# One written order from the query products to the second group of the attention's output projection, and other task rates

## The chip, the cores and the metric

The kernel runs on one core of one Trainium2 chip. The metric is the device time of one execution in microseconds (us). The kernel before takes 2666.85 us, the median of three runs (2665.67 to 2668.78). The execution that was profiled took 2665.4 us; its trace spans 2663.6 us from the first to the last instruction. All times inside the trace are counted from the start of that span.

## The reference, cut to what matters

One step of a one-layer decoder on 512 prompt tokens and 8 sample (decode) tokens, all in fp32:

```
x += W_out [ norm(RG-LRU group) ; headnorm(mLSTM group) * o ]
x += CrossAttn(RMSNorm(x), memK, memV)      4 heads of 512 over 256 memory tokens
x += W_down relu(RMSNorm(x) W_up)^2
y  = RMSNorm(x)
```

For the prompt tokens the memory's keys and values are products of `mem_prompt` with `w_mk` and `w_mv`. Each of the 8 decode tokens has keys and values of its own, which come ready from the caches `cache_mem_k` and `cache_mem_v`. Both kinds of tokens go together through the weights `w_cq` (queries) and `w_co` (output projection).

## The kernel before, in words

**Tiles.** The 520 tokens are the columns, 128 features the rows of a tile. An fp32 product is made of three matmuls on rounded parts: a weight is cast to a high part `whi` on ScalarE (L129 or L138), and VectorE subtracts to get the low part `wlo` (L130 or L146); activations are split likewise. High and low parts of weights have three buffers each, so the cast for a job waits until TensorE is done with the job three before it.

**Jobs.** A job is one weight block of 128 x 1024 and its matmuls. The list `jobs` holds them in the order in which TensorE makes them. The part that matters here is:

- 32 jobs of the query products (`w_cq`), 4 heads of 4 column blocks of 2 jobs; 48 matmuls each
- 64 jobs of the memory's keys and values: keys and values of head 0, of head 1, keys of heads 2 and 3, values of heads 2 and 3; eight jobs each. The matmuls of one such job take about half the time of a query job. Their cost is given as `MCOST`
- the output projection `w_co`: 4 plain jobs (`plain_pair`, 48 matmuls each), then seven groups of seven products of 24 matmuls (`quad_jobs`, a Strassen-like scheme over 2 x 2 blocks, in the order P1 P2 P6 P5 P7 P3 P4). `n_early` is the number of the first plain job; the first group is `n_early + 4` to `n_early + 10`, the second `n_early + 11` to `n_early + 17`

In a group P1, P6, P7 and P4 add into one PSUM accumulator, P5 and P3 into another. After each product the result so far is added to `x` (L1452), and the next product into the same accumulator waits for that addition. Four weight sums are formed on VectorE in a group (L1310). When a pair of rows of `x` is complete, a task `fact_pair` forms four sums of it for the MLP (L1271, L1272, L1253), and `sums_out` splits and stores them (L1282, L1284). The first `fact_pair` waits seven steps.

**Tasks.** Work beside the jobs is written as generators. `step_tasks` is called once in each job and advances every task:

```
t[2] += 1.0 if t[1] is None else t[1] * cost
while t[2] > 0.999:
    t[2] -= 1.0
    next(t[0])
```

The decode tokens' attention is one such task, `attn_decode_all`, with rate `DRATE`. It walks through 64 items: for each head eight items of keys (L1018) and eight of values (L1025), one per decode token; the order is K0 K1 V0 K2 V1 K3 V2 V3. An item's 512 KB are loaded by GpSimd's queue (L986, L993) four items ahead, and VectorE reduces them: for an item of values, four instructions at L1025. When the last value item of a head is done, the prompt's task of that head (`attn_prompt`) may make its second product, probabilities times values (TensorE, L224), copy the four results out of PSUM (L1217, with the decode columns from `od` at L1218), and split them into `fo` (L799, L800), which the output projection reads. For each pair of them a task `o_sums` forms four differences (L889), splits them (L899, L900) and stores them by GpSimd's queue into `odram` (L902, L903); `block_out` starts it, for the first four pairs with a rate of its own. `o_loads` brings the stored differences back as `to` for the groups of the output projection (L915, SyncE's queue) and makes those of the last two pairs itself (L889, L799, L800). GpSimd's queue also stores the finished memory keys and values; all that it issues goes out in the order in which it is written.

**What sets the order.** In a block `tc.manual_schedule()` each engine issues the block's instructions in the order in which the program writes them. Outside such a block, and between the instructions of two blocks, a planner decides by priorities. In a manual block `run_jobs(..., fixed=True)` writes for job i: the loads, the cast of job i+2, one step of the tasks, the low part of job i+2, the matmuls of job i, the result's evacuation. With `low_first` the low part comes ahead of the tasks' step. In the kernel before there are three such blocks near the change: from the first query job to the second plain job (with the loop that empties the task list), the third and fourth plain job, and the first group. Between the first and the second stand, to the planner, the release of the early SBUF pools, the opening of the late one, four weight loads held back for it, and the start of `o_loads`. From the second group on the planner orders everything but the very last two products.

Of the kernel before, what the change touches and what calls it, by code (L numbers as in the profile page):

```python
# [14 lines left out]
PSUM = bass.MemoryType.PSUM  # L15
# [22 lines left out]
EVAC = 100  # L38
EARLY = 10
PRE = 1  # L40
DRATE = 1.45
MCOST = 0.35


@with_exitstack
def tile_trunk(ctx: ExitStack, tc: tile.TileContext, a, o):
# [9 lines left out]
    early_sb, early_ps = (ctx.enter_context(ExitStack()) for _ in range(2))  # L56
# [3 lines left out]
    late = {}  # L60
# [26 lines left out]
    def halves(t):  # L87
        return t.rearrange("p (h c) -> p h c", h=2)
# [14 lines left out]
    jobs = []  # L103
# [7 lines left out]
    def w_load(i):  # L111
        if "fetch" in jobs[i] or "raw" in jobs[i] or "w" in jobs[i]:
            return
        jobs[i]["raw"] = w_raw(jobs[i]["src"])

    def w_fetch(i):
        if i < len(jobs) and "fetch" in jobs[i]:
            jobs[i]["fetch"]()
# [22 lines left out]
    def w_low(i):  # L141
        if "w" in jobs[i]:
            return
        raw, hi = jobs[i].pop("cast")
        lo = wpool.tile([P, 8, P], F32R, tag="wlo", name=nm("wlo"))
        V.tensor_tensor(out=lo, in0=raw, in1=hi.bitcast(F32), op=ALU.subtract)  # L146
        jobs[i]["w"] = hi, lo

    def start(gen, rate=None):

        tasks.append([gen, rate, 0.0])

    def step_tasks(cost=1.0):
        for t in list(tasks):
# [3 lines that stand above are left out]
                try:  # L158
                    next(t[0])
                except StopIteration:  # L160
                    tasks.remove(t)
                    break

    def run_jobs(first, last, fixed=False, low_first=False):


        n = len(jobs)
        for i in range(first, last):
            with tc.high_priority(offset=AHEAD):
                for k in (i + 3, i + 4)[1 if i else 0:]:  # L170
                    if k < n:
                        w_load(k)
                w_fetch(i + FETCH)
                if i + 2 < n:
                    (w_cast if fixed else w_split)(i + 2)
            j = jobs[i]
            if "pre" in j:
                j["pre"]()
            if low_first:
                w_low(i + 2)  # L180
            step_tasks(j.get("cost", 1.0))
            if fixed and i + 2 < n:
                w_low(i + 2)
            j["mm"](*j.pop("w"))
            if "post" in j:
                with tc.high_priority(offset=EVAC):
                    j["post"]()
        while last == n and tasks:
            step_tasks()
# [602 lines left out]
    def pair_slot(name):  # L792
        return slot(name, (P, 2, HT), F32R)

    def split_to(out, src, g=None):

        hi, lo = out[:, 0], out[:, 1]
        if g is None:
            S.copy(hi, src)  # L799
            V.tensor_tensor(out=lo, in0=src, in1=hi.bitcast(F32), op=ALU.subtract)  # L800
        else:
            S.activation(hi, src, AF.Copy, scale=g)
            V.scalar_tensor_tensor(out=lo, in0=src, scalar=g, in1=hi.bitcast(F32),
                                   op0=ALU.mult, op1=ALU.subtract)
# [66 lines left out]
    o_even, o_last = {}, []  # L871

    def block_out(t, n):
        fo[n] = [pair_slot("fo") for _ in range(2)]
        for hf in range(2):
            split_to(fo[n][hf], t[:, HALF[hf]])
        i = n // 2
        if n % 2 == 0:
            o_even[i] = t
        elif i < 6:  # L880
            start(o_sums(i, o_even.pop(i), t, i < 4), 2.2 if i < 4 else None)
        else:
            o_last.append((i, o_even.pop(i), t))

    def diffs(t0, t1):

        b11, b12, b21, b22 = t0[:, HALF[0]], t0[:, HALF[1]], t1[:, HALF[0]], t1[:, HALF[1]]
        for j, out, p, q in ((4, b11, b12, b11), (5, b12, b22, b12), (6, b22, b22, b11), (7, b21, b21, b22)):
            V.tensor_tensor(out=out, in0=p, in1=q, op=ALU.subtract)  # L889
            yield j, out  # L890

    def o_sums(i, t0, t1, slowly):

        for n, _ in enumerate(diffs(t0, t1)):
            if n == 3 or slowly and n == 1:
                yield
        for t, js in ((t1, (7, 6)), (t0, (4, 5))):
            hi = pair_slot("oh")
            S.copy(hi, halves(t))  # L899
            V.tensor_tensor(out=halves(t.bitcast(F32R)), in0=halves(t), in1=hi.bitcast(F32), op=ALU.subtract)  # L900
            for k, j in enumerate(js):
                stream_load(odram[i][j - 4, :, 0], hi[:, k].bitcast(F32))  # L902
                stream_load(odram[i][j - 4, :, 1], t[:, HALF[k]])  # L903
            if slowly:
                yield

    def o_loads():

        for i in range(KB // 2):
            to[i][1], to[i][2], to[i][3] = fo[2 * i][0], fo[2 * i + 1][0], fo[2 * i + 1][1]  # L910

        def fetch(j):
            for i in range(len(odram)):
                to[i][j] = pair_slot("to")
                load(to[i][j].bitcast(F32), odram[i][j - 4])  # L915

        def make(j, of):
            for i, d, got in of:
                while j not in got:
                    k, x = next(d)  # L920
                    got[k] = x
                to[i][j] = pair_slot("to")
                split_to(to[i][j], got[j])

        last = [(i, diffs(t0, t1), {}) for i, t0, t1 in o_last]
        o_last.clear()
        fetch(6)
        make(6, last[0:1])
        yield
        make(6, last[1:2])  # L930
        fetch(4)
        yield
        make(4, last)
        fetch(5)
        yield
        make(5, last)
        yield
        fetch(7)
        make(7, last)
# [6 lines left out]
    def ev_q(h, j):  # L946
        def ev(ps):
# [5 lines left out]
            if h == 0 and j == 3:  # L953
                start(attn_decode_all(), DRATE)
            if h == 0 and j == 0:
# [132 lines left out]
    def split_later(parts):  # L1088

        for t, hi, lo in parts:  # L1090
            yield
            S.copy(hi, t)
            V.tensor_tensor(out=lo, in0=t, in1=hi.bitcast(F32), op=ALU.subtract)

    def mk_jobs(h, j):
# [3 lines left out]
        def mm(g, wh, wl):  # L1099
            if g == 0:  # L1100
                box["ps"] = mm_tile()[:, 0, 0:NMEM]
            for i in range(8):
                k = g * 8 + i
                xh, xl = mact[k]
                for wi, (w, x) in enumerate(((wh, xh), (wh, xl), (wl, xh))):
                    PE.matmul(box["ps"], w[:, i, :], x, start=(k == 0 and wi == 0),  # L1106
                              stop=(k == KB - 1 and wi == 2))

        def post():
# [7 lines left out]
            if j == 3:  # L1117
                start(attn_prompt(h))
        js = [dict(src=a["w_mk"][n, g], cost=MCOST, mm=lambda wh, wl, g=g: mm(g, wh, wl)) for g in range(2)]
        js[-1]["post"] = post  # L1120
        return js

    def mv_jobs(h):
# [16 lines left out]
        def post():  # L1140
# [5 lines left out]
            start(split_later(mvx[h]))  # L1146
        js = [dict(src=a["w_mv"][h, g], cost=MCOST, mm=lambda wh, wl, g=g: mm(g, wh, wl)) for g in range(8)]
        js[-1]["post"] = post
# [490 lines left out]
    n_early = len(jobs)  # L1639
    jobs += projection("w_co", dx[0], dx[1], "ssf", fo, to, x2_done, fact_split, False)  # L1640

    held = [jobs[n_early + 4 + i].pop("fetch") for i in range(2)]
# [18 lines left out]
    with tc.manual_schedule():  # L1661
        run_jobs(n_cq, n_early + 2, True)
        while tasks:
            step_tasks()
    early_sb.close()
    late["sb"] = ctx.enter_context(tc.tile_pool(name="late", bufs=2, reuse_waits="tile"))
    for fetch in held:
        fetch()
    start(o_loads())
    with tc.manual_schedule():  # L1670
        run_jobs(n_early + 2, n_early + 4, True, True)
    early_ps.close()
    late["mm"] = ctx.enter_context(tc.tile_pool(name="lmm", bufs=3, space=PSUM, reuse_waits="tile"))
    late["aux"] = ctx.enter_context(tc.tile_pool(name="laux", bufs=2, space=PSUM, reuse_waits="tile"))
    with tc.manual_schedule():
        run_jobs(n_early + 4, n_early + 11, True, True)
    run_jobs(n_early + 11, len(jobs) - 2)
    assert not tasks
    with tc.manual_schedule():
        finish(*jobs[-2:])  # L1680
# [103 lines left out]
```

## Time and profile before

| what | value |
|---|---|
| median of three runs | 2666.85 us (2665.67 to 2668.78) |
| profiled execution | 2665.4 us, span 2663.6 us |
| TensorE busy (matmul) | 2627.0 us, 99% |
| VectorE busy | 2219.9 us, 83% |
| ScalarE busy | 1296.9 us, 49% |
| query products | 749 to 936 us |
| memory keys and values | 936 to 1168 us |
| plain jobs of the output projection, rest of the attention | 1168 to 1204 us |
| its first group | 1204 to about 1234 us |

TensorE is busy nearly everywhere, so what a change in this part of the kernel is worth is read from the few places where TensorE waits, or where its granted clock is below full speed. In the rows a matmul's own time is about 0.28 us, but they overlap: their starts stand 0.12 us apart for 260 columns and 0.23 us for 512. The same holds, less strongly, for VectorE and ScalarE, so the distance of two starts is what an instruction costs its engine.

### The profile page before, as it was taken

How to read it: one execution, taken by the hardware profiler on the slowest of the kernel's cores; microseconds unless marked ns; L12 is line 12 of the kernel's file. 1: busy time of each engine (PE TensorE's matmuls, PEld its weight loads, DVE VectorE, ACT ScalarE, POOL GpSimd, SP SyncE). 2: the span in 40 equal slices, each digit the busy share in tenths (PEclk: the TensorE clock that was granted, in tenths of full speed). 3: DMA queues.
4: the chain of work that ended last, by engine and by line, in shares of the span. 5: the costliest groups of instructions: out<-in, count | busy, mean ns of one | idle time of the engine just before them, and what ended most of it. 6: DMA issues, size and time to landing. Idle time of an engine off the chain costs nothing.

```text
span 2663.6 us, 52729 instructions
## 1 busy us (share of the span) xinstructions
PE 2627.0 (99%) x21250; PEld 2589.5 (97%) x21250; DVE 2219.9 (83%) x3729; ACT 1296.9 (49%) x1779; POOL 134.1 (5%) x232
## 2 busy tenths in 40 slices
PE   9999999999999999998999999999999999999997
PEld 9999999999999998988999999999999999999997
DVE  6787685887864568878999999999999988998898
ACT  5646455553453245544575555555553333333344
POOL 0010000000001213320000000000000000000001
PEclk9999999999999999999999999999999999999999
DMA  5354353576456778877687565565579666555642
GB/s 205 106 187 152 112 169 103 175 240 223 141 182 202 275 266 302 293 254 269 224 273 243 199 213 185 199 212 188 196 244 330 216 223 216 183 169 191 211 132 89
DMA packets 243847, 545.43 MB, mean 205 GB/s; under 512 B 26015, under 2 KB 98367, under 8 KB 243603
## 3 DMA queue, kind: packets, MB, share of 16 engines
q1 hardware_dynamic: 222354, 468.55, 51.8%
q0 software_dynamic: 21248, 73.51, 8.0%
q8 instruction: 167, 2.74, 0.4%
q14 instruction: 78, 0.63, 0.1%
HBM read 436.39 MB, written 105.72 MB: 204 GB/s over the span
## 4 chain that ended last, share of the span: by engine, by line
PE 87%; issue 4%; DVE 4%; DMA 2%; ACT 1%; POOL 0%; SPq 0%; POOLq 0%; DVEq 0%; ACTq 0%
PE mm L1340 51%; PE mm L205 22%; PE mm L1137 3%; PE aux L1340 2%; PE aux L224 2%; PE mm L1106 2%; PE mm L1383 2%; DVE wlo L146 1%; PE aux L730 0%; DMA wraw<-in_w_mk 0%; PE aux L663 0%; PE aux L659 0%; DMA wraw<-in_w_in 0%; DMA hc<-r 0%; DMA A<-in_w_co 0%
## 5 line engine op out<-in xcount | busy, mean ns | idle before, releaser
L129 ACT CAST whi<-wraw 128x1024 fp32r<-128x1024 f32 x392 | 411.9, 1051 | 633.1 <-PE mm L1340 414.4
L1340 PE MATMUL mm<-ha,whi 128*128 128x260 f32 x3584 | 644.1, 283 | 2.1 <-DVE X L1521 1.1
L130 DVE TENSOR_TENSOR wlo<-wraw,whi 128x1024 fp32r<-128x1024 f32 x392 | 478.3, 1220 | 120.1 <-ACT whi L129 118.4
L1340 PEld LDWEIGHTS mm<-ha,whi 128*128 128x128 f32 x3584 | 551.0, 188 | 3.0 <-DVE X L1521 1.5
L1340 PE MATMUL mm<-ha,wlo 128*128 128x260 f32 x1792 | 505.1, 282 | 0.6 <-DVE wlo L130 0.6
L1340 PE MATMUL mm<-ta,whi 128*128 128x260 f32 x2320 | 418.6, 282 | 0.0
L1340 PEld LDWEIGHTS mm<-ta,whi 128*128 128x128 f32 x2320 | 355.9, 188 | 0.0
L1340 PEld LDWEIGHTS mm<-ha,wlo 128*128 128x128 f32 x1792 | 337.1, 188 | 1.0 <-DVE wlo L130 1.0
L1340 PE MATMUL mm<-ta,wlo 128*128 128x260 f32 x1160 | 326.4, 281 | 0.0
L1340 PE MATMUL mm<-fa,whi 128*128 128x260 f32 x1488 | 268.6, 282 | 0.0
L205 PE MATMUL mm<-xh,whi 128*128 128x260 f32 x1280 | 265.0, 287 | 0.0
L205 PE MATMUL mm<-xl,whi 128*128 128x260 f32 x1280 | 259.1, 283 | 0.0
L205 PE MATMUL mm<-xh,wlo 128*128 128x260 f32 x1280 | 258.1, 282 | 0.0
L129 ACT CAST whi<-A 128x1024 fp32r<-128x1024 f32 x138 | 144.9, 1050 | 193.2 <-PE mm L1340 143.0
L1340 PEld LDWEIGHTS mm<-fa,whi 128*128 128x128 f32 x1488 | 228.5, 188 | 0.0
L138 ACT CAST whi<-wraw 128x1024 fp32r<-128x1024 f32 x104 | 109.0, 1050 | 238.4 <-PE mm L205 76.9
L1340 PEld LDWEIGHTS mm<-ta,wlo 128*128 128x128 f32 x1160 | 218.4, 188 | 0.0
L1340 PE MATMUL mm<-fa,wlo 128*128 128x260 f32 x744 | 209.4, 281 | 0.0
L1521 DVE TENSOR_TENSOR X<-mm,X 128x260 f32<-128x260 f32 x448 | 170.8, 421 | 42.0 <-PE mm L1340 40.5
L205 PEld LDWEIGHTS mm<-xh,whi 128*128 128x128 f32 x1280 | 198.5, 188 | 1.4
L205 PEld LDWEIGHTS mm<-xh,wlo 128*128 128x128 f32 x1280 | 198.2, 189 | 0.2
L205 PEld LDWEIGHTS mm<-xl,whi 128*128 128x128 f32 x1280 | 197.8, 189 | 0.3
(439 smaller groups left out, 5236.1 us busy)
## 6 DMA issues: line engine op xcount, KB each, us to landing
ha<-hc SPq DMA_DIRECT2D x224, 260.0 KB
wraw<-in_w_in SPq DMA_DIRECT2D x80, 512.0 KB
wraw<-in_w_up SPq DMA_DIRECT2D x66, 512.0 KB
wraw<-in_w_down SPq DMA_DIRECT2D x64, 512.0 KB
A<-in_w_down SPq DMA_DIRECT2D x64, 512.0 KB
A<-in_w_up SPq DMA_DIRECT2D x62, 512.0 KB
hc<-hhi SPq DMA_DIRECT2D x32, 910.0 KB
hc<-r SPq DMA_DIRECT2D x32, 910.0 KB
```

Source lines behind the costliest of these rows:

```text
L129: S.copy(hi, raw)
L130: V.tensor_tensor(out=lo, in0=raw, in1=hi.bitcast(F32), op=ALU.subtract)
L138: S.copy(hi, raw)
L146: V.tensor_tensor(out=lo, in0=raw, in1=hi.bitcast(F32), op=ALU.subtract)
L205: PE.matmul(ps[:, hf, 0:HT], w[:, j, :], x[:, HALF[hf]], start=(k == 0 and wi == 0), stop=(k == n - 1 and wi == 2))
L224: PE.matmul(out, u, v, start=first and i == 0, stop=last and i == 2)
L1106: PE.matmul(box["ps"], w[:, i, :], x, start=(k == 0 and wi == 0), stop=(k == KB - 1 and wi == 2))
L1137: PE.matmul(box["ps"][:, i], x[:, ms], w[:, j], start=(k == 0 and wi == 0), stop=(k == KB - 1 and wi == 2))
L1340: PE.matmul(out, w[:, j, :], x[:, b], start=(new and k == 0 and wi == 0), stop=(p == LAST[acc] and k == per - 1 and wi == 2), skip_group_c ...
L1383: PE.matmul(ps[mp][:, hf, 0:HT], w[:, j, :], x[hf][:, b], start=(kp == 0 and j == 0 and wi == 0), stop=(kp == 1 and j == 7 and wi == 2))
L1521: V.tensor_tensor(out=x, in0=c, in1=x, op=ALU.add)
```

## The change

`DRATE` goes from 1.45 to 1.6 and `MCOST` from 0.35 to 0.32, the rate of the first four `o_sums` tasks from 2.2 to 2.5. The steps of the decode task in a query job (cost 1) go from 1.45 to 1.6; in a job of the memory's keys or values from 0.5075 to 0.512; those of the `o_sums` tasks there from 0.77 to 0.80. The three manual blocks become one, which takes in what stood between them and goes on through the second group (to `n_early + 17`).

```
-DRATE = 1.45
-MCOST = 0.35
+DRATE = 1.6
+MCOST = 0.32
...
-            start(o_sums(i, o_even.pop(i), t, i < 4), 2.2 if i < 4 else None)
+            start(o_sums(i, o_even.pop(i), t, i < 4), 2.5 if i < 4 else None)
...
         run_jobs(n_cq, n_early + 2, True)
         while tasks:
             step_tasks()
-    early_sb.close()
-    late["sb"] = ctx.enter_context(tc.tile_pool(name="late", bufs=2, reuse_waits="tile"))
-    for fetch in held:
-        fetch()
-    start(o_loads())
-    with tc.manual_schedule():
+        early_sb.close()
+        late["sb"] = ctx.enter_context(tc.tile_pool(name="late", bufs=2, reuse_waits="tile"))
+        for fetch in held:
+            fetch()
+        start(o_loads())
         run_jobs(n_early + 2, n_early + 4, True, True)
-    early_ps.close()
-    late["mm"] = ctx.enter_context(tc.tile_pool(name="lmm", bufs=3, space=PSUM, reuse_waits="tile"))
-    late["aux"] = ctx.enter_context(tc.tile_pool(name="laux", bufs=2, space=PSUM, reuse_waits="tile"))
-    with tc.manual_schedule():
-        run_jobs(n_early + 4, n_early + 11, True, True)
-    run_jobs(n_early + 11, len(jobs) - 2)
+        early_ps.close()
+        late["mm"] = ctx.enter_context(tc.tile_pool(name="lmm", bufs=3, space=PSUM, reuse_waits="tile"))
+        late["aux"] = ctx.enter_context(tc.tile_pool(name="laux", bufs=2, space=PSUM, reuse_waits="tile"))
+        run_jobs(n_early + 4, n_early + 18, True, True)
+    run_jobs(n_early + 18, len(jobs) - 2)
```

## The prediction

> **What bounds the kernel now.** I read the page's first lines, then the busy times of the stages from the query products to the end of the output projection, then who TensorE (PE) waited for there.
>
> ```profile
> span 2663.6 us, 52729 instructions
> PE 2627.0 (99%) x21250; PEld 2589.5 (97%) x21250; DVE 2219.9 (83%) x3729; ACT 1296.9 (49%) x1779; POOL 134.1 (5%) x232
> ```
> ```profile
> core 0: us, PE busy (x) PEld busy (x) DVE busy (x) ACT busy (x) POOL busy (x), PEclk, DMA share, GB/s
> 749.00:936.00 187.00, 187.00 (x1560) 186.44 (x1559) 102.58 (x236) 61.19 (x89) 25.77 (x39) 1.00 0.63 216
> 936.00:1168.00 232.00, 226.83 (x1461) 203.05 (x1460) 180.62 (x431) 115.84 (x205) 59.82 (x99) 1.00 0.82 282
> 1168.00:1204.00 36.00, 32.50 (x221) 30.63 (x220) 30.12 (x89) 15.90 (x42) 12.12 (x22) 0.91 0.69 236
> 1204.00:1237.00 33.00, 25.88 (x194) 25.50 (x193) 24.75 (x38) 16.29 (x25) 0.00 (x0) 0.84 0.98 344
> 1237.00:1254.00 17.00, 16.75 (x140) 16.75 (x141) 16.97 (x24) 9.27 (x11) 0.00 (x0) 1.00 0.69 223
> 1254.00:1355.00 101.00, 101.00 (x847) 101.00 (x846) 97.40 (x139) 63.68 (x88) 0.00 (x0) 1.00 0.68 226
> ```
> ```profile
> 1168.33 0.64 PE L1383 MATMUL mm<-fo,whi 128*128 128x260 f32 x4
> 1192.15 1.76 PE L1383 MATMUL mm<-fo,whi 128*128 128x260 f32 x4 [3.47 <-ACT fo L799]
> 1203.82 0.43 PE L1340 MATMUL mm<-fo,whi 128*128 128x260 f32 x2
> 1216.55 0.77 PE L1340 MATMUL mm<-to,whi 128*128 128x260 f32 x2 [6.81 <-ACT to L799]
> ```
> ```profile
> 1191.00:1198.00 7.00, 5.85 (x24) 5.54 (x25) 5.97 (x16) 5.11 (x17) 3.98 (x8) 0.52 0.97 331
> 1211.00:1222.00 11.00, 5.45 (x25) 5.48 (x26) 8.57 (x17) 6.37 (x12) 0.00 (x0) 0.53 0.98 345
> ```
> ```profile
> 1165.70 2.79 PE aux L224 x12
> 1237.25 117.67 PE mm L1340 x982
> ```
>
> PE has nothing to give beside the queries (187 of 187 us). Where the change acts, it waits 3.47 us for the last `fo` and 6.81 us ahead of the first group's P6, and after either wait its clock is granted at half (0.52 and 0.53).
>
> I count from T0 = 1168.33, the first plain product. A matmul of 260 columns costs 117.67/982 = 0.12 us, so a plain job (48) 5.75, a product of a group (24) 2.88, and head 3's probabilities times values (24 of L224) 2 x 2.79 = 5.6. From T0 to P1 (1203.82) 35.5 us pass for 4 x 5.75 + 5.6 = 28.6 of work: 6.9 lost, 3.47 in the wait, most of the rest by the half clock behind it. Group 2 ends at 1237.25 + (982 - 5 x 168) x 0.12 = 1254.3. From P1 on that is 50.4 us for 14 x 2.88 = 40.3: 10.1 lost, 6.81 waiting, some 2.5 by the clock. **17.0 us** is all that can be won here.
>
> **What holds PE.** VectorE's queue.
>
> ```profile
> 1189.91 0.42 DVE L1025 CUSTOM_DVE_ANT_0 kv<-kv,kv 128x256 f32<-128x256 f32 x1
> ...
> 1191.29 1.30 DVE L900 TENSOR_TENSOR o<-o,oh 128x520 fp32r<-128x520 f32 x2
> ...
> 1199.14 1.22 DVE L1310 TENSOR_TENSOR A<-A,A 128x1024 f32<-128x1024 f32 x1
> ...
> 1209.87 0.69 DVE L1444 TENSOR_TENSOR xr<-mm,xr 128x520 f32<-128x520 f32 x1
> 1211.35 1.11 DVE L1253 TENSOR_TENSOR r<-r 128x260 f32<-128x260 f32 x3 [0.80 <-ACT r L1272]
> 1213.58 1.24 DVE L1284 TENSOR_TENSOR r<-r,hhi 128x1040 fp32r<-128x1040 f32 x1 [1.12 <-ACT hhi L1282]
> 1214.74 0.69 DVE L268 TENSOR_TENSOR ssf<-ssf,sq 128x520 f32<-128x520 f32 x1
> 1215.35 0.76 DVE L800 TENSOR_TENSOR to<-o,to 128x260 fp32r<-128x260 f32 x2
> 1216.03 0.42 DVE L1452 TENSOR_TENSOR x<-mm,x 128x260 f32<-128x260 f32 x1
> 1216.37 1.21 DVE L146 TENSOR_TENSOR wlo<-A,whi 128x1024 fp32r<-128x1024 f32 x1
> 1217.50 0.76 DVE L800 TENSOR_TENSOR to<-o,to 128x260 fp32r<-128x260 f32 x2
> ```
>
> The last decode item ends at 1191.3 = T0+23.0, and `fo` of head 3 stands behind it. P6 starts at 1216.55, just behind the end of P1's addition (L1452, 1216.45), not behind L799, which the row names: P6 adds to the same accumulator. Ahead of that addition stand L1253 and L1284, the first `fact_pair`, which the planner drew forward from the second group; they wait on ScalarE by turns (0.80, 1.12). Starts in these rows price VectorE's work: 260 columns 0.34, 520 columns 0.61, 1024 (a weight's low part or a weight sum) 1.13, L1284 1.16, an item of values 1.38.
>
> **Part 1, the rates.** By the rule of `step_tasks`, each query job after the decode task's start makes 1.6 steps in place of 1.45; 24 such jobs make 3.6 steps more, of which the wait for each head's query rows swallows some: 26 items are done at the end of the queries, in place of 24. They cost 2 x 1.38 = 2.8 us beside a VectorE that is busy 102.58 of 187 us; without that cover they would cost PE those 2.8. Beside keys and values the rate stays (0.5075 to 0.512), so the lead of two items persists. Its main effect is that head 2's last item falls in the second of the last eight value jobs, not in the sixth: its product, four copies, eight splits into `fo`, and the differences of pairs 4 and 5 move from the first plain jobs and the loop behind them into those value jobs. Head 3's last item moves only one step, from the third to the second of the emptying loop.
>
> I wrote down VectorE's queue for that order. In the last five value jobs it can't begin head 2's `fo` before TensorE's product: half of that (2.8) and four jobs of 12 matmuls (2.8 each, as L224) lie behind the job that frees ScalarE, 13.9 us ahead of T0; a cast, a copy and a split there make it 11.5. Then come items 57 and 58 (2.8), eight splits (2.7), eight differences (2.7), two L900 (1.2), four low parts (4.5), and some 2.7 waiting for ScalarE's copies: 16.6, so it is 5.1 us late at T0. Items 59 to 63 (6.9), two L900, two halves of head 3's values (1.2), two low parts (2.3) follow: item 63 ends at T0+16.7, where before it was T0+23.0. Two prices:
> - TensorE is ready for head 3's product at T0+11.5, but the halves of its values come at T0+12.2 and, behind item 62, T0+15.3: it waits 3.3 us.
> - The `fo` wait of 3.47 and its half clock go: the plain job that needs `fo` then starts at T0+20.4 and comes to it at T0+23.3; it is there from T0+17.9.
>
> P1 starts at 28.6 + 3.3 = T0+31.9. This part loses 3.3 in place of 6.9.
>
> **Part 2, one order.** `fact_pair` 0 goes back to its own place, steps 8 to 11, in group 2. The path to P6 is now: the last plain job ends at T0+31.9; sum into `xr` 0.65, ScalarE's square and L268 1.3, then the two weight sums of P6 (L1310, 1.13 each and a wait between), which the planner had put ahead at 1199 and which now stand where they are written; the cast, the low part, two splits, P1's addition.
>
> ```profile
> L138 ACT CAST whi<-wraw 128x1024 fp32r<-128x1024 f32 x9 | 9.3, 1049 | 10.0 <-PE mm L1383 4.9 <-DVE wraw L1310 2.0 <-PE mm L1340 1.6
> ...
> L1282 ACT CAST hhi<-r 128x1040 fp32r<-128x1040 f32 x6 | 6.3, 1058 | 2.3 <-DVE r L1253 2.3
> ```
>
> That is 0.7 + 1.3 + 2.5 + 1.05 + 1.15 + 0.7 + 0.4 = 7.8 and some 0.3 of handing over: T0+40.0, where P6 is due at T0+37.6. P6 loses 2.4, P7 and P3 of the group 1.4 in the same way (a weight sum, a cast, a low part, an addition). Group 1: 3.9.
>
> Group 2 now holds `fact_pair` 0 and 1. VectorE's sum there: seven low parts and four weight sums 12.4, seven additions 2.4, two L268 1.2, twice four sums and an L1284 5.0: 21.0 us beside 20.1 of TensorE, and in written order it must also wait for ScalarE's casts about 1 us each time. By the queue: P6 2.4, P7 0.7, P3 2.1, in all 5.3; before, the planner lost 0.25 there (16.75 of 17). At its end VectorE is 4 us late.
>
> **Sum.** 3.3 + 3.9 + 5.3 = 12.5 in place of 17.0.
>
> **What the trace doesn't show, from both sides.** Items 62 and 63 are loaded from GpSimd's queue, in the new order behind the stores of pairs 4 and 5; 63 is issued at about T0+11.8 (pair 5's first L900 ends at T0+7.2, then eight stores of 0.54).
>
> ```profile
> 1188.61 0.54 POOL L902 DMA_DIRECT2D od<-oh  x1
> ...
> kv<-in_V POOLq DMA_DIRECT2D x4, 512.0 KB, 7.8
> od<-oh POOLq DMA_DIRECT2D x8, 130.0 KB, 4.0
> ...
> out_mv<-mv POOLq DMA_DIRECT2D x2, 256.0 KB, 2.6
> kv<-dp POOLq DMA_DIRECT2D x1, 512.0 KB, 5.3
> ```
>
> Landing takes 2.6 to 7.8 us in this stretch. At 2.6 item 63 waits for nothing; at 7.8 it is 4.3 late and P6 with it. I take 5.3, the same queue and size: 1.7 more at P6, whose wait becomes 4.2.
>
> The clock: the waits of 3.47 and 6.81 halved it, at 2.5 to 3.0 us each; this one of 1.81 did not:
>
> ```profile
> 1031.77 0.50 PE L1137 MATMUL mm<-wlo,mh 128*128 128x512 f32 x1 [1.81 <-DVE wlo L146]
> ...
> 1029.00:1036.00 7.00, 5.19 (x30) 4.18 (x29) 7.00 (x17) 4.09 (x6) 4.70 (x9) 1.00 0.89 303
> ```
>
> My waits of 2.4 to 4.2 lie between; 0 to 5.5 us. I take one halving, behind P6: 2.5. Together 12.5 + 1.7 + 2.5 = 16.7, 0.3 less than before. The Trainium skill ("TensorE: Matmul & The Clock Gate", Part 1) says that the clock is halved after an idle window of about 3.4 us; the two halved waits agree. By that rule my other waits of 2.1 to 2.5 would not halve it; that is the second rival below.
>
> The rest: the phase of items beside keys and values shifts by half a job, where PE now loses 5.2 us (226.83 of 232): -2 to +2. VectorE's 4 us at the end of group 2: 0 to 4, as it has 3.6 us to spare until 1355 (97.40 of 101). I take 0 for both, as PE lost nothing there with VectorE as full.
>
> So the profiled execution would take about 2665.4 - 0.3. The median of the three runs stands 1.45 above it, so this is 2666.5; I say **2666**, the likeliest case's own range 2662 to 2671. About 0.2% (5.3 us) is what can be told from no change.
>
> **Rivals.**
> - *Faster.* VectorE reaches T0 on time, because the value jobs leave it more room than I counted (180.62 of 232 busy speaks for it; that head 2's product comes late in them, against). Then the 3.3 at head 3's product go, item 63 lands in time and no wait reaches 3.4: 12.5 - 3.3 = 9.2 lost, 7.8 less than before: 2659. Chance 0.25.
> - *The clock stays whole*, items land at once: 12.5 lost, 4.5 less: 2662, still within 0.2%. The row at 1031 speaks for it; that the waits here follow one another closely, against. Chance 0.13.
> - *Slower.* VectorE's lateness at the end of group 2 passes into the later groups. It decides where the lag is over the 3.6 us to spare. Then the third group loses the 4 again, and a second wait over 3.4 halves the clock once more (2.5 to 3): 16.7 + 4 + 3 = 23.7, 6.7 more than before: 2673.5. For it: VectorE is 96% busy to 1355, and group 2 has two `fact_pair`s. Against: the planner kept PE at 101.00 of 101. Chance 0.2.
> - *The order does nothing*, since the planner draws work of the third group forward into the block as it did with `fact_pair` 0; the rates alone give 3.6: in the forecast's range.
>
> **How the numbers follow.** Forecast 0.42 with the last rival, then 0.25, 0.13, 0.2. Faster by over 0.2% is the first rival and a little of the second, 0.27; slower 0.21; within 0.52. Eight in ten: 2658.5 to 2673.5.
>
> **What would show it.** Right: L1025 ends about 6 us earlier after the first plain product; no wait for `fo` L799; L224 of head 3 waits for the values' low half; L1253 and L1284 stand behind P1's addition; waits of 2 to 4 us at P6 of both groups; VectorE over 95% busy in group 2. Wrong: TensorE without a gap in group 2, or a gap over 4 us in group 3, or the clock whole all through.

## The result, and the profile after

The changed kernel takes **2677.72 us**, the median of six runs (2675.72 to 2678.85), beside 2666.57 for the kernel before in six runs of its own (2665.67 to 2669.71). The ratio is 1.0039, with a 95% interval of 1.0026 to 1.0051: **slower by 11 us**, a small loss but one clear of the noise. The forecast was 2666, with 2658.5 to 2673.5 for eight cases in ten, so the time lies above the whole range.

The first lines of the page of the profiled execution (2678.28 us):

```profile
span 2676.5 us, 52715 instructions
...
PE 2630.5 (98%) x21250; PEld 2591.9 (97%) x21250; DVE 2221.0 (83%) x3729; ACT 1296.0 (48%) x1779; POOL 134.0 (5%) x232
```

The busy times by stage, bounded at this kernel's own first products of each stage; the columns are those of the table in the prediction:

```profile
core 0: us, PE busy (x) PEld busy (x) DVE busy (x) ACT busy (x) POOL busy (x), PEclk, DMA share, GB/s
749.00:936.00 187.00, 187.00 (x1560) 186.44 (x1559) 105.06 (x244) 61.29 (x89) 27.75 (x42) 1.00 0.64 224
936.00:1171.60 235.60, 228.46 (x1462) 204.72 (x1461) 181.78 (x434) 119.23 (x219) 58.69 (x97) 0.99 0.79 272
1171.60:1207.80 36.20, 30.75 (x218) 28.59 (x217) 26.50 (x80) 13.72 (x29) 11.21 (x20) 0.91 0.75 255
1207.80:1233.50 25.70, 21.88 (x171) 21.70 (x170) 20.19 (x31) 10.68 (x16) 0.00 (x0) 0.93 0.89 313
1233.50:1266.30 32.80, 24.32 (x170) 23.45 (x169) 22.55 (x31) 13.51 (x19) 0.00 (x0) 0.84 0.59 189
1266.30:1367.00 100.70, 100.70 (x843) 100.61 (x842) 97.51 (x139) 62.66 (x87) 0.00 (x0) 1.00 0.69 228
```

Group 2 of the output projection, the fifth row, takes 32.8 us where its products need 20.1, and its clock is at 0.84. No engine is full there: VectorE is busy 22.55 of those 32.8 us, ScalarE 13.51. The waits of TensorE, and the first rows of the first plain product (T0), of group 1 and of group 2, in the timeline of the same execution:

```profile
1111.32 1.05 PE L1201 MATMUL aux<-ident,p 128*128 128x128 f32 x4 [2.78 <-DVE p L1188]
...
1171.61 0.28 PE L1383 MATMUL mm<-fo,whi 128*128 128x260 f32 x1
...
1184.48 0.50 PE L224 MATMUL aux<-pTh,mvl 128*128 128x512 f32 x1 [0.75 <-DVE mvl L1093]
1190.16 0.80 PE L224 MATMUL aux<-pTh,mvl 128*128 128x512 f32 x1 [4.70 <-DVE mvl L1093]
...
1207.78 0.40 PE L1340 MATMUL mm<-fo,whi 128*128 128x260 f32 x2
...
1217.49 0.71 PE L1340 MATMUL mm<-to,whi 128*128 128x260 f32 x2 [3.82 <-ACT to L799]
...
1233.47 0.40 PE L1340 MATMUL mm<-fo,whi 128*128 128x260 f32 x2
...
1241.38 0.71 PE L1340 MATMUL mm<-to,whi 128*128 128x260 f32 x2 [2.00 <-DVE x L1452]
1253.23 0.47 PE L1340 MATMUL mm<-fo,whi 128*128 128x260 f32 x2 [1.49 <-DVE x L1452]
1260.31 0.80 PE L1340 MATMUL mm<-fo,whi 128*128 128x260 f32 x2 [3.99 <-ACT whi L138]
1262.11 0.80 PE L1340 MATMUL mm<-to,whi 128*128 128x260 f32 x2 [1.00 <-DVE x L1452]
```

The wait for `fo` is gone, P6 of group 1 (1217.49) waits 3.82 in place of 6.81. In group 2 P6 (1241.38), P3 (1253.23) and P4 (1260.31 and 1262.11) wait, 8.5 us in all, where the kernel before had no wait of a microsecond.

I measure stages by the start times of their first products, the same ones in every trace: keys and values from the first product of `w_mk` to T0; T0 to P5 of group 1; group 2 from its P1 to the next; groups 3 to 7; the up projection from its first product to the first of the down projection. The kernel before has 231.81, 53.56, 20.92, 100.43 and 645.38 us; the changed one adds +3.30, -3.20, **+11.93**, +0.19 and +0.35, with +0.4 behind them. That is the 12.9 us between the two spans.

**Why P4 waits.** The chain in the same timeline, ScalarE's and VectorE's rows:

```profile
1244.78 1.06 ACT L1282 CAST hhi<-r 128x1040 fp32r<-128x1040 f32 x1 [0.40 <-DVE r L1253]
1249.29 1.05 ACT L138 CAST whi<-wraw 128x1024 fp32r<-128x1024 f32 x1 [3.44 <-DVE wraw L1310]
1257.31 1.06 ACT L1282 CAST hhi<-r 128x1040 fp32r<-128x1040 f32 x1 [6.97 <-DMA td<-hhi]
1258.27 1.04 ACT L138 CAST whi<-A 128x1024 fp32r<-128x1024 f32 x1
...
1259.34 1.23 DVE L146 TENSOR_TENSOR wlo<-A,whi 128x1024 fp32r<-128x1024 f32 x1 [6.25 <-ACT whi L138]
```

The second pair's cast (L1282) can't start before the store of the first pair's high parts has read the `hhi` tile, of which there is one buffer. P4's weight cast stands behind it on ScalarE, its low part behind that on VectorE. And SyncE, in the same timeline, with the line for it from the view of waits (group 2 and the start of group 3):

```profile
1235.56 0.44 SPq L1298 DMA_DIRECT2D A<-in_w_co  x1
1249.24 0.33 SPq L108 DMA_DIRECT2D wraw<-in_w_co  x1
1249.62 0.42 SPq L1298 DMA_DIRECT2D A<-in_w_co  x1
1250.14 0.38 SPq L1286 DMA_DIRECT2D td<-hhi  x1
```
```profile
SPq L108 <- DVE wraw L1310: 13.2, 1, 13.2
```

The first pair's cast was done at 1245.8, but its store went out at 1250.14, 4.3 us later, since in the written order two weight loads of group 3 stand ahead of it, and the first of them waited 13.2 us for a weight buffer that VectorE frees with P3's weight sum. From its issue the store then took another 7.2 us until the second pair's cast could start at 1257.31. A wait for a buffer on one queue thus held another engine through a third.

### The profile page after: what moved, and what is told of

Its sections match the earlier page's. It is cut to its first block, busy times and chain, and to the rows that moved or that the text cites. A ratio compares the mean times of both kernels' runs of the same rounds, so it can differ in the third digit from the quotient of the medians.

```text
span 2676.5 us, 52715 instructions
## 1 busy us (share of the span) xinstructions
PE 2630.5 (98%) x21250; PEld 2591.9 (97%) x21250; DVE 2221.0 (83%) x3729; ACT 1296.0 (48%) x1779; POOL 134.0 (5%) x232
## 4 chain that ended last, share of the span: by engine, by line
PE 89%; DVE 5%; DMA 2%; issue 2%; ACT 2%; POOL 0%; SPq 0%; POOLq 0%; ACTq 0%; DVEq 0%
PE mm L1340 54%; PE mm L205 22%; PE aux L1340 2%; PE mm L1137 2%; PE mm L1106 2%; PE aux L224 2%; PE mm L1383 2%; DVE wlo L146 1%; DMA wraw<-in_w_mv 1%; DVE wlo L130 1%; PE aux L730 0%; ACT whi L129 0%; ACT whi L138 0%; PE aux L663 0%; PE aux L659 0%
```

## The experiments

The runs are to tell five theories apart:

- A: each half of the change has its own place. The rates act ahead of T0 and on the `fo` wait; the written order pays in group 1 and costs in group 2.
- B: the rates' lag on VectorE is carried into group 2.
- C: joining the blocks costs.
- D: VectorE has too little room in group 2, whoever orders it.
- E: the cost is in the written order itself.

Each run stands beside runs of the kernel before that were made with it; the brackets give the ratio's 95% interval. The table at the end of this section has the stages of all runs.

**Rates alone.** The kernel before with `DRATE` 1.6, `MCOST` 0.32 and 2.5 for the `o_sums` tasks.

> The three new rates, with the three written blocks and the planner's stretch of the kernel before. Theory A (each half of the change has its own place): the keys and values stage ends 3.4 us later, as in the changed kernel, since all of it lies ahead of the blocks' boundaries; between the first plain product of the attention's output projection and P5 of group 1 it gains 0 to 3.5, for the wait for the gathered `fo` tile goes; group 2 stays in the planner's hands and keeps its time. Sum 2666.5 to 2670. Theory B (the rates' lag on VectorE is carried into group 2 and makes the 12 us there): 2675 to 2679, with the late cast of the second pair in group 2 here too.

2670.57 us beside 2666.79 for the kernel before (1.0012, 1.0002 to 1.0021). Group 2 keeps its time (+0.79), so B falls. In place of the `fo` wait stands one of 1.98 us ahead of head 3's product, P6 still waits 6.81, and T0 to P5 gains only 0.23. The 3.8 us of the medians are not where A put them: see the two last runs.

**Order alone.** The changed kernel with 1.45, 0.35 and 2.2.

> The one written order up to the end of group 2, with the rates of the kernel before. Theory A: keys and values stage at 0.0 us, the first products to P5 of group 1 between 0 and -3.5, and group 2 loses 7 to 12 us, with the store of the first pair's high parts waiting behind a weight load on SyncE's queue: 2670 to 2679. Theory B (the rates bring the loss): 2663 to 2667.

2677.69 us, as slow as the whole change (1.0041, 1.0027 to 1.0055). Group 2 loses 12.17 us with the same two rows, ScalarE's in the timeline and SyncE's in the view of waits:

```profile
1254.36 1.06 ACT L1282 CAST hhi<-r 128x1040 fp32r<-128x1040 f32 x1 [7.04 <-DMA td<-hhi]
```
```profile
SPq L108 <- DVE wraw L1310: 13.5, 1, 13.5
```

A holds: the 12 us belong to the written order of group 2, with either set of rates.

**The joined order, ending with group 1.**

```
-        run_jobs(n_early + 4, n_early + 18, True, True)
-    run_jobs(n_early + 18, len(jobs) - 2)
+        run_jobs(n_early + 4, n_early + 11, True, True)
+    run_jobs(n_early + 11, len(jobs) - 2)
```

> The changed kernel with the one written order ending with group 1, where the last block of the kernel before ended; the planner has group 2. Theory A: +3.4 from the keys and values stage, -3.2 from the first products to P5 of group 1, group 2 as before: 2666 to 2669, so within 2 us of the rates alone plus the merged blocks. Theory C (joining the blocks at the memories' boundary costs the time, wherever the order ends): 2675 to 2679.

2669.84 us, 3.0 above the kernel before (1.0009, 1.0000 to 1.0018). Group 2 is at -0.83, so C falls too. But T0 to P5 is now 1.54 slower: the -3.2 that A had put there do not come from joining the blocks. P6 of group 1 waits 6.81 as before, with the first pair's four sums and L1284 ahead of P1's addition (L1452) again, in VectorE's rows of the timeline:

```profile
1209.20 1.11 DVE L1253 TENSOR_TENSOR r<-r 128x260 f32<-128x260 f32 x3 [0.80 <-ACT r L1272]
1211.43 1.24 DVE L1284 TENSOR_TENSOR r<-r,hhi 128x1040 fp32r<-128x1040 f32 x1 [1.13 <-ACT hhi L1282]
...
1218.66 0.42 DVE L1452 TENSOR_TENSOR x<-mm,x 128x260 f32<-128x260 f32 x1
```

What pays in group 1 is that a written group 2 keeps the planner from drawing that pair forward.

**The stores on another queue.** The changed kernel with both stores of `sums_out` issued by GpSimd (`stream_load` for `load`).

> The changed kernel with the two stores of each pair's sums (`td`) on GpSimd's queue in place of SyncE's, so that they no longer stand behind the weight loads of group 3. Theory A (the chain of group 2's P4: weight load waits for a buffer on SyncE, the store behind it, the single `hhi` buffer, ScalarE's cast): the cast of the second pair starts some 6 us earlier, the 3.99 us wait ahead of P4's products goes with its half clock, and the time falls by 4 to 8, to 2670 to 2674. Theory D (VectorE is full in group 2 and is late by itself): within 1.5 us of the changed kernel, 2676 to 2679.

2672.57 us, 5 less than the changed kernel (1.0020, 1.0011 to 1.0030). The timeline, ScalarE's rows and TensorE's wait in P4:

```profile
1252.57 1.06 ACT L1282 CAST hhi<-r 128x1040 fp32r<-128x1040 f32 x1 [2.49 <-DVE r L1284]
1253.54 1.04 ACT L138 CAST whi<-A 128x1024 fp32r<-128x1024 f32 x1
...
1257.38 0.51 PE L1340 MATMUL mm<-to,whi 128*128 128x260 f32 x2 [1.05 <-DVE x L1452]
```

The first pair's store goes out at 1246.12 here and lands 3.4 us later, so the cast waits for VectorE's L1284 and no longer for the store; counted from group 2's P1 it comes 4.4 us earlier, the wait of 3.99 and its half clock are gone, and group 2 loses 6.03 in place of 11.93. The chain is shown, and it is half of group 2's loss. The other half is P6 (2.04 and the half clock behind it), P3 (1.51) and what is left at P4 (1.05).

**The first pair later.** The same, with the first `fact_pair` waiting 14 steps in place of 7.

> The changed kernel with `td`'s stores on GpSimd's queue, as in the run before, and the first pair's start put off from 7 to 14 steps, so that its written place is in group 3. Theory D (what is left of group 2's loss is VectorE's own 21 us of work beside 20.1 us of products): without the first pair's 2.5 us the group loses 6.0 - 2.5 to 6.0 - 4 us: 2668 to 2670. Theory E (the loss is the way back and forth between VectorE and ScalarE in the written order at P6 and P3, whatever the pairs do): group 2 still loses 5 to 6 us, 2671 to 2674.

2677.86 us, 5 slower than its partner: both theories missed. Group 2 loses only 2.96, all of it at P6, but groups 3 to 7 lose 6.38 (two waits of 1.4 and 1.6 us, and the clock at half for 6.8). The pair's work was moved, not hidden. It has four executions only; in the profiled executions groups 2 to 7 make 1.8 of the 5 us, the up projection 2.0.

**The written order up to P2 of group 2**, with the new rates and with the old:

```
-        run_jobs(n_early + 4, n_early + 18, True, True)
-    run_jobs(n_early + 18, len(jobs) - 2)
+        run_jobs(n_early + 4, n_early + 13, True, True)
+    run_jobs(n_early + 13, len(jobs) - 2)
```

> The changed kernel, SyncE's stores as they are, with the written order ending after P2 of group 2, so that the first pair's scaling is still in the written order behind group 1 but the planner places the rest of group 2. Theory E (written order costs in group 2, and pays in group 1 only by keeping the first pair out of it): from the first plain product to P5 of group 1 it gains 2.4 to 3.2 over the kernel before, group 2 loses 0 to 3: 2663 to 2668. Theory D (VectorE has too little room in group 2 once it holds both pairs, whoever orders it): group 2 loses 5 to 6 here too, 2669 to 2673.

> The same end of the written order after P2 of group 2, with the rates of the kernel before. If the rates bring nothing in either direction (theory A after the first runs, in which keys, values and the wait for `fo` came out within 2 us with both), this lies within 2 us of the run with the new rates. If the new rates gain by the wait for `fo`, it is 3 us slower; if the new rates cost by their phase beside keys and values, up to 3 us faster.

2671.51 us (1.0014, 1.0005 to 1.0023) with the new rates, 2667.59 (1.0003, 0.9994 to 1.0012) with the old. Group 1 gains 3.05 and 2.29, group 2 loses 2.94 and 2.99, all at P6, whose two weight sums still stand as written, and groups 3 to 7 some 1.5. Neither theory has it whole: E is right that the planner spares P3 and P4, and what group 1 gains P6 of group 2 gives back. Between the two medians the rates cost 3.9 us, though the stages that they should act on differ by no more than 1.0.

**Up to P5 of group 2**, with the stores on GpSimd's queue (`n_early + 15`).

> The changed kernel with `td`'s stores on GpSimd's queue and the written order ending after P5 of group 2. Both pairs' scalings, casts and the first pair's sums stand as written, the planner takes over at P7. Theory E: P6 of group 2 loses its 1.1 us and half a clock, 2.7 in all, as in the run with the stores alone, and the 1.7 at P3 and the rest go: 2668 to 2671. Theory D: as the run with the stores alone, 2671 to 2674.

2674.40 us (1.0029, 1.0018 to 1.0041), and group 2 loses 7.79, more than with the whole group written. A planner that takes over behind P5, with both pairs half done, doesn't recover the loss; E falls here. How much of what is left at P6 and P3 is VectorE's lack of room (D) and how much the written order (E) stays open.

**The first pair two steps later, nothing else.** One number of the kernel before, then the same in the joined order to the end of group 1 with the old rates, then with the new.

```
-        start(fact_pair(i, x0, x1, 1 if i else 7))
+        start(fact_pair(i, x0, x1, 1 if i else 9))
```

> The kernel before, its blocks, its rates, with one number changed: the first pair's start is put off from 7 to 9 steps, which lets the planner place its four sums behind P6's addition in group 1 and its L1284 in group 2; the two weight sums of P6 stay early. If the first pair ahead of P1's addition is what makes the 6.81 us wait at P6 (its four sums, its L1284 and the two waits on ScalarE between are 1.5 + 1.24 + 0.80 + 1.12 = 4.6), group 1 gains 3 to 6 with the clock, group 2 loses up to 1: 2661 to 2664. If the wait is held by something else, 2666 to 2669.

> The joined written order up to the end of group 1, with the rates of the kernel before and the first pair put off to 9 steps. Theory E (keeping the first pair out of P6's way is the whole gain, the written order itself gives none): P6's two weight sums stand as written behind P1's square, so it gains less in group 1 than the three blocks with the same 9 steps: 1 to 3 for the first plain product to P5, group 2 at 0 to +1: 2663 to 2667. If joining the blocks gains by itself, it is as fast as the three blocks with 9 steps or faster, 2660 to 2663.

> The run before with the three new rates. The pair of runs with the written order up to P2 of group 2 gave 3.9 us more with the new rates, and the rates alone 3.8 us more than the kernel before, though no stage of the profiled executions showed so much. If the rates really cost, this is 2 to 5 us slower than its partner with the old rates; if not, within 2 us.

Beside 2668.67 us for the kernel before these take **2664.66** (0.9987, 0.9978 to 0.9996), **2664.11** (0.9988, 0.9979 to 0.9996) and 2666.72 (0.9997, 0.9988 to 1.0006). The first two beat the kernel before, by 4.0 and 4.6 us, and so the changed one. Group 2 is whole in all three; for the first, its row of the busy times and VectorE's row ahead of P6 of group 1 in the timeline:

```profile
1232.40:1252.80 20.40, 20.40 (x173) 20.40 (x172) 20.37 (x27) 11.22 (x13) 0.00 (x0) 1.00 0.75 234
```
```profile
1214.94 0.43 DVE L1452 TENSOR_TENSOR x<-mm,x 128x260 f32<-128x260 f32 x1 [2.06 <-DMA x<-dx]
```

Group 1 gains 1.6 where I expected 3 to 6: P6 still waits 5.27, since P1's addition, no longer behind the pair, now waits for the load of `x`. From T0 to the end of group 2 the profiled execution gains 2.2 of the 4 us; the others have no place in its stages. Joining the blocks adds nothing that can be told (0.55 us between the medians). The new rates cost 2.6 us once more.

**What the rates cost, and where.** Three pairs say 3.8, 3.9 and 2.6 us, a fourth (the changed kernel beside the order alone) nothing; a fifth follows below with 1.4. No wait that I found explains this: keys and values are 0.9, 1.0 and 3.3 us longer with the new rates in the first three, but 3.9 longer in the fourth and 1.8 shorter in the fifth. The one stage that is longer by over 1 us in each of the others, and by 0.3 in the fourth, is the up projection, where TensorE never waits (in the second pair the down projection, too, is 2.2 us longer). First rows of it and of the down projection, kernel before:

```profile
1354.77 0.40 PE L1383 MATMUL mm<-fa,whi 128*128 128x260 f32 x2
...
2000.14 0.41 PE L1340 MATMUL mm<-ha,whi 128*128 128x260 f32 x2
```

and with the rates alone:

```profile
1357.39 0.40 PE L1383 MATMUL mm<-fa,whi 128*128 128x260 f32 x2
...
2006.02 0.40 PE L1340 MATMUL mm<-ha,whi 128*128 128x260 f32 x2
```

645.4 and 648.6 us for the same products. The group products that read `fa` start on the mean every 119.16 and 120.27 ns (119.69 in the changed kernel), and this is no jitter: each of the 168 matmuls of a group has its own distance to the next, 114 to 127 ns, which repeats through 29 groups of the stage, and kernels whose `fa` tiles lie at the same addresses in the built program share the mean. The rates change which tiles of the slot pool `fa` and `ta` get. The last two runs exchange the places of the two halves of `fa` (the loop over the halves in `fact_split` runs backwards), with TensorE's order unchanged.

> The joined order to the end of group 1, the first pair at 9 steps, the old rates, and in `fact_split` the second half split ahead of the first, so that the two halves of each `fa` tile change places in the slot pool; TensorE's instructions stay in the same order. In the twelve kernels so far the mean start-to-start time of the up projection's group products over 30 chunks is one of four values, 119.16, 119.45, 119.69 and 120.27 ns, and the kernels with the same places for `fa` and `ta` share a value; its partner has 119.17. If the places set the pace, this kernel's value moves to another by 0.3 ns or more, and the stretch from the first up product to the first down product by 1 us or more, either way. If the pace is the execution's own or goes with the order of the instructions, the value stays at 119.16 to 119.18 and the stretch at 645.4.

> The same exchange of the halves' places with the new rates; its partner has 120.27 ns and 648.2 us from the first up product to the first down product. If the places set the pace, the value moves by 0.3 ns or more, most likely down; if not, it stays at 120.27.

2665.20 us (0.9992, 0.9982 to 1.0002) and 2666.56 (0.9998, 0.9988 to 1.0008), beside 2668.10. The mean distance of those products moved from 119.17 to 119.32 ns and from 120.27 to 119.61 ns, the stage from 645.36 to 644.99 us and from 648.20 to 647.79. The first pair moved less than the 0.3 ns that I had asked for, the second more, and neither stage moved by 1 us. In the second the stage did not follow, since the other group products, which read `ta`, slowed from 119.44 to 119.75 ns. So the places may have a part in it, but 2.8 us between the two sets of rates remain in this stage: their cause **stays open**. Nor do the new rates always bring it: the changed kernel, which has them too, takes 645.7 us there.

| run | median, us | beside before | keys, values | T0 to P5 | group 2 | groups 3-7 | up |
|---|---|---|---|---|---|---|---|
| changed kernel | 2677.72 | +11.2 | +3.30 | -3.20 | +11.93 | +0.19 | +0.35 |
| rates alone | 2670.57 | +3.8 | +0.93 | -0.23 | +0.79 | +0.07 | +3.25 |
| order alone | 2677.69 | +10.9 | -0.55 | -2.34 | +12.17 | +0.16 | +0.05 |
| to group 1 | 2669.84 | +3.0 | -0.82 | +1.54 | -0.83 | +0.03 | +2.88 |
| stores on GpSimd | 2672.57 | +5.8 | +0.99 | -2.60 | +6.03 | +1.56 | +0.36 |
| and pair at 14 | 2677.86 | +11.2 | -0.63 | -3.11 | +2.96 | +6.38 | +2.39 |
| to P2 of group 2 | 2671.51 | +4.8 | +1.09 | -3.05 | +2.94 | +1.50 | +2.00 |
| same, old rates | 2667.59 | +0.9 | +0.11 | -2.29 | +2.99 | +1.66 | +0.72 |
| to P5, stores on GpSimd | 2674.40 | +7.7 | -0.42 | -2.91 | +7.79 | +0.03 | +2.07 |
| before, pair at 9 | 2664.66 | -4.0 | +0.76 | -1.64 | -0.82 | +0.11 | -0.01 |
| joined, pair at 9 | 2664.11 | -4.6 | -1.27 | -2.03 | -0.83 | +0.23 | -0.01 |
| same, new rates | 2666.72 | -2.0 | +1.99 | -3.23 | -0.82 | +0.39 | +2.82 |
| halves exchanged, old rates | 2665.20 | -2.9 | +1.51 | -1.95 | -0.83 | 0.00 | -0.39 |
| halves exchanged, new rates | 2666.56 | -1.5 | -0.32 | -3.37 | -0.82 | +0.05 | +2.41 |

The second column of numbers sets each median beside that of the kernel before run with it; the stages, of one profiled execution each, stand beside those of the kernel before's profiled execution. The medians are of 4 to 11 runs. What is left out here (the rest of group 1, within 0.3 but +1.3 in the two last runs with the new rates; the down projection; the start) and the executions themselves make up some 3 us at most between the two: the start of the kernel up to the queries, which is the same in all of them, took between 748.7 and 751.0 us.

## Why the prediction was wrong, by its own steps

*Part 1.* The first sign it named, two more decode items in the queries, came: VectorE does 244 instructions there in place of 236, and TensorE is busy 187 of 187. So did the end of the `fo` wait, and the wait of head 3's product for its values' low halves. But that wait was 0.75 + 4.70 = 5.45 us where I had 3.3. The rows of the two last items say why:

```profile
1179.40 0.72 POOL L993 DMA_DIRECT2D kv<-in_V  x1 [0.26 <-issue]
...
1188.03 0.42 DVE L1025 CUSTOM_DVE_ANT_0 kv<-kv,kv 128x256 f32<-128x256 f32 x1 [2.46 <-DMA kv<-in_V]
...
1193.99 0.43 DVE L1025 CUSTOM_DVE_ANT_0 kv<-kv,kv 128x256 f32<-128x256 f32 x1 [3.88 <-DMA kv<-in_V]
```

Item 62's load, too, stands behind the stores on GpSimd's queue and took 8.6 us to land, over the 7.8 of my upper bound. That 7.8 was a misreading: it is the median of four loads, and the slowest of them in the kernel before took 9.5. And I had priced a wait for item 63 alone, and at P6. VectorE lost 2.46 us between the two halves of head 3's values, and the last L1025 (three more behind 1193.99, 0.35 apart) ended at T0+23.8, where it was T0+23.0 before and I had T0+16.7. With the halved clock behind it, T0 to P1 loses 36.2 - 28.6 = 7.6 us where I had 3.3 and the kernel before has 6.9: the rates only changed which wait stands there.

*Part 2, group 1.* Right in kind: the first pair went back behind P1's addition, P6 waits 3.82 (near my 2.4 + 1.7, but in part by luck: the 1.7 stood for a late load, and VectorE waits for no load there), and P1 to the next group's P1 loses 25.7 - 20.2 = 5.5 us, where I had 8.1; the 1.4 at P7 and P3 did not come. The run that ends the order with group 1 adds that only the written group 2 sends the pair back.

*Part 2, group 2: **the step that failed**.* "P6 2.4, P7 0.7, P3 2.1, in all 5.3." P6 and P3 are there, 2.00 and 1.49. But I had added up VectorE's work and one microsecond for each cast, and taken ScalarE's and SyncE's queues for free. The written order puts two weight loads ahead of the store of `hhi`, the load waits for a buffer, and the store, the single `hhi`, ScalarE's cast and P4 wait behind it: 5 us of waiting in P4 and half a clock for 6.8. The run with the stores on GpSimd's queue took that out. What group 2 still loses there, 26.95 - 20.16 = 6.8 us, is close to my 5.3 and the 1.7 of one window at half clock, but partly by luck: P6 and P3 are 2.04 and 1.51, the 0.7 at P7 didn't come, and P4's 1.05 was not in my sum (whose three parts, besides, make 5.2). The sign that I had set for this group, VectorE over 95% busy, failed with it (22.55 of 32.8). No rival had this link either; the slower one put its 7 us in group 3, by VectorE's lag, and group 3 has no gap. A loss of that size in groups 3 to 7 came only in the run with the first pair at 14 steps.

*The clock.* I took one halving, 2.5 us. There were five stretches, behind the waits of 2.78, 4.70, 3.82, 2.00 and 3.99, seven windows of 3.41 us in all. My bounds, 1.81 without and 3.47 with, held; I chose the wrong end for the waits near 2. A window at half clock costs half of its 3.41, 1.7 us.

*Keys and values.* I took 0 and -2 to +2; this execution lost 3.3, by the wait of 2.78 us at 1111.32 and its half clock. None of the eight other profiled executions with the new rates has that wait (-0.8 to +2.0), so the rates alone do not bring it; what did is open. *The up projection*, 0.35 here and up to 3.25 with the rates alone, I had not listed at all, as nothing waits there.

The sum from T0 was 16.7 us lost; it is 7.6 + 5.5 + 12.7 = 25.8. Of the 9.1 missing, 7.4 are group 2 and 4.3 part 1, while group 1 came out 2.6 better than I had it: two errors that cancelled in part.

## To carry over

When an order is written out past the point where a planner had it, walk every queue in that order, the DMA queues first: a load that waits for a buffer holds all that is written behind it, and a single-buffered tile behind such a store carries the wait to an engine that no sum of work shows to be full. Ask first which one instruction of the planner's order costs, and move that: two steps of delay for one task gained 4 us, 0.15%, where the whole written order lost 11. And where a group of matmuls waits by pieces of 2 us, price the clock behind each.

## What the runs showed of the hardware

**The clock.** The same wait of 1.82 us halves the clock in one execution and not in another. The wait and the granted clock (0.50) of the 3.4 us behind it, with the rates alone:

```profile
1032.29 0.71 PE L1137 MATMUL mm<-wlo,mh 128*128 128x512 f32 x1 [1.82 <-DVE wlo L146]
```
```profile
1028.90:1032.30 3.40, 1.58 (x8) 0.94 (x6) 3.31 (x6) 0.63 (x1) 1.61 (x3) 1.00 0.97 374
1032.40:1035.80 3.40, 3.40 (x9) 2.63 (x10) 2.52 (x5) 3.40 (x7) 2.05 (x4) 0.50 0.77 239
```

and in the changed kernel, at 1.00:

```profile
1031.16 0.50 PE L1137 MATMUL mm<-wlo,mh 128*128 128x512 f32 x1 [1.82 <-DVE wlo L146]
```
```profile
1031.20:1034.60 3.40, 3.40 (x18) 2.92 (x19) 1.94 (x4) 3.40 (x6) 1.47 (x3) 1.00 0.87 305
```

From the queries to the up projection the half stretches of every trace last 3.41 or 6.83 us, one in the kernel before 10.24, and within a trace their starts stand a whole number of 3.41 us apart (1111.7, 1186.8, 1217.6, 1241.5 and 1258.5 in the changed kernel: 22, 9, 7 and 5 of them). Laid out on that grid, the first wait lies whole in one window; the second is cut by a boundary at 1029.8 into 0.5 and 1.3. Over the 15 profiled executions, from keys and values to the up projection, each of the 43 windows at full clock with 1.82 us of waiting or more is followed by a half one, and none of the 41 with 0.9 to 1.6; of the seven between, two are. So what counts is the waiting inside one window, about half of its length. The Trainium skill ("TensorE: Matmul & The Clock Gate", Part 1) says that the window runs freely and lasts 3413 ns, and the trace agrees with both; that it takes an idle window, as the page has it and as I read it for the second rival, the runs don't show: half of one is enough. The 3.47 us wait of the kernel before, which I took to agree with that rule, held no idle window either: its half stretch starts at 1191.24, and that boundary cuts the wait into 2.56 and 0.92.

**The pace of products.** Products of one shape that wait for nothing start 114 to 127 ns apart by their place in the program, and a whole stage can be 3 us of 645 longer for it; what sets the distance was not found.
